# Seven block products for eight: half of the k-tiles of chunk pairs in a two-layer diffusion trunk

## The chip, the cores and the metric

One core of a Trainium2 chip. The metric is device time of one launch in microseconds (us). Matmuls run on TensorE (PE), elementwise work on VectorE (DVE), ScalarE (ACT) and GpSimd (POOL), DMAs are issued by SyncE (SP).

## The reference

640 tokens (128 context, 512 latent) of 2048 features go through two layers. Each layer modulates the RMS-normed tokens, projects them to several streams, mixes them in two branches, multiplies by a SiLU gate, projects back and adds the residual:

```python
shift, scale, gate = jnp.split(jax.nn.silu(cond) @ ada_w[l] + ada_b[l], 3, axis=-1)
h = rms_norm(x, norm_g[l]) * (1.0 + scale) + shift
y = mixer(h @ w_in)            # layer 0: windowed attention || gated linear attention
                               # layer 1: neighbourhood attention || spatial-gating MLP
x = x + gate * ((y * silu(gp)) @ w_out[l])
...
return rms_norm(x, final_norm_g)
```

The projections are 2048 to 5664 (layer 0), 2048 to 7168 (layer 1) and 2048 to 2048 (each output projection).

## The kernel before

Activations lie with features on partitions: 16 k-tiles of 128 features by 640 tokens. Each fp32 value is kept as a high and a low part (`ah`, `al`), each weight likewise (`whi`, `wlo`). A *chunk* is 128 output features. `mm_k` runs one k-tile of it: hi x high, hi x low, lo x high, each for two halves of 320 tokens, the first with two more columns in front for the shift (322). A chunk is thus 16 x 6 = 96 matmuls; `chunk` runs them and then evacuates the two PSUM banks `pj`. There are 133 chunks: 45 into layer 0 (one of 96 rows), 16 out of it, 56 into layer 1 and 16 out. All activation matmuls are issued at line 334, plain fp32 transposes at 339, the start's at 803; DVE, ACT and POOL instructions go through a recorder and all carry line 187.

Weights come as 512 KB loads of 8 k-tiles (`wraw`; 256 KB for the first chunks). ACT rounds them to `whi`, POOL subtracts to get `wlo`, in a ring of three such units (`wpump`).

The order on every engine is fixed when the program is built: a planner (`Pace`) keeps a clock per engine, `tick` runs after each k-tile and advances tasks (attention heads, evacuations, splits), `need(flag)` stands for a point where the next work of TensorE requires a task to be done. `ada_task` is the lowest task: it computes the modulation rows of the later parts on DVE, a multiply-and-sum of 512 columns of weights against one of two condition rows, both in SBUF (`adas`).

Where one layer's output is the next one's input, the last two and the first two chunks are run by `pair`: both chunks for one half of the tokens, then both for the other, with weights kept in an extra pool (`tphi`, `tplo`). The very last pair splits the tokens at 352 (`LAST`) instead of 320, so that its second half is shorter; `final` then computes the last norm of each half.

After layer 0's windowed attention come its eight last gates, then the first output projection, then layer 1: the MLP's `u` chunks, its `v` chunks, the first two gates, 24 chunks for eight neighbourhood heads, 14 gates, the last output projection. Small products (attention scores, transposes) use four other banks, `sm`.

## Time and profile before

| | us |
|---|---|
| median of three runs | 2222.53 (2221.79 to 2223.55) |
| the profiled execution, its own time | 2221.39 |
| its span, first to last instruction | 2219.6 |
| mean granted TensorE clock | 0.994 |

A group row reads: line, engine, operation, output<-inputs, shape, count | busy us, mean ns of one | idle time of the engine just before, and what ended it. Matmul rows overlap, so the spacing of their starts says more than their length.

### The profile page before, as it was taken

The page shows a single profiled execution, that of the slowest core. Times are in us where ns is not written, and L with a number is a line of the kernel's source. Part 1 is how long each engine was busy: PE and PEld are TensorE (multiplying, and loading weights), DVE is VectorE, ACT ScalarE, POOL GpSimd, SP SyncE. Part 2 cuts the span into 40 slices and gives each one's busy share as a digit, 9 for nine tenths or more (in the row PEclk, how much of TensorE's full clock was granted, in tenths as well). Part 3 has the DMA queues.
Part 4 walks back from the last instruction along what each step waited for, and adds up shares of the span by engine and source line. Part 5 has one row for each costly group of instructions (what it writes and reads, how often), then busy time and mean ns, then how long its engine had stood idle before and what let it go on. Part 6 is the DMA issues. An engine that isn't in the chain of part 4 may idle for free.

```text
span 2219.6 us, 36587 instructions
## 1 busy us (share of the span) xinstructions
PE 2166.6 (98%) x14770; PEld 2094.9 (94%) x14770; DVE 1171.6 (53%) x2525; ACT 714.6 (32%) x1403; POOL 767.9 (35%) x375
## 2 busy tenths in 40 slices
PE   7999999999999999999999999999999999999996
PEld 4789999899899899999999999999999999999996
DVE  1348788887878787978778814222222221140004
ACT  4334344343333334122522222233233322242222
POOL 3433233223222143556433332222323323334453
PEclk9999999999999999999999999999999999999998
DMA  9944343335334243666445522222222222222333
GB/s 374 348 159 128 126 139 104 113 126 174 102 112 131 93 144 121 200 218 200 144 147 191 185 67 76 82 73 81 77 89 75 79 67 75 87 82 88 100 103 114
DMA packets 116377, 288.26 MB, mean 130 GB/s; under 512 B 13232, under 2 KB 25328, under 8 KB 116208
## 3 DMA queue, kind: packets, MB, share of 16 engines
q1 hardware_dynamic: 114736, 284.49, 38.9%
q8 instruction: 116, 1.90, 0.3%
q10 hardware_dynamic: 1472, 1.43, 0.2%
q14 instruction: 53, 0.43, 0.1%
HBM read 270.39 MB, written 12.86 MB: 128 GB/s over the span
## 4 chain that ended last, share of the span: by engine, by line
PE 82%; DVE 9%; issue 3%; DMA 3%; ACT 2%; SPq 1%; POOL 0%; DVEq 0%; ACTq 0%; POOLq 0%
PE pj L334 69%; PE sm L334 10%; DVE adas L187 3%; DVE arena L187 3%; PE sm L339 2%; DVE Y L187 2%; PE sm L803 2%; ACT arena L187 1%; DMA Y<-ada 1%; SPq L364 1%; DMA adas<-crow_s 1%; DMA arena<-xT 0%; DMA wraw<-w_even 0%; DMA adas<-ada 0%; DVE actl L187 0%
## 5 line engine op out<-in xcount | busy, mean ns | idle before, releaser
L187 POOL TENSOR_TENSOR wlo<-wraw,whi 128x1024 fp32r<-128x1024 f32 (+2 forms) x260 | 630.1, 2425 | 1157.4 <-ACT whi L187 979.4
L334 PE MATMUL pj<-acth,whi 128*128 128x322 f32 (+1 forms) x3824 | 919.0, 317 | 1.1 <-DVE Y L187 1.1
L334 PE MATMUL pj<-actl,whi 128*128 128x322 f32 (+1 forms) x3824 | 894.5, 310 | 0.0
L334 PE MATMUL pj<-acth,wlo 128*128 128x322 f32 (+1 forms) x3824 | 894.3, 310 | 0.0
L334 PEld LDWEIGHTS pj<-acth,whi 128*128 128x128 f32 x3824 | 644.5, 190 | 5.3 <-issue 1.7
L334 PEld LDWEIGHTS pj<-acth,wlo 128*128 128x128 f32 x3824 | 649.1, 189 | 0.0
L334 PEld LDWEIGHTS pj<-actl,whi 128*128 128x128 f32 x3824 | 646.7, 189 | 0.1
L187 ACT ACTIVATE whi<-wraw 128x1024 fp32r<-128x1024 f32 (+2 forms) x260 | 262.2, 1010 | 331.9 <-issue 179.0
L187 DVE TENSOR_TENSOR arena<-pj,rstd 128x320 f32<-128x320 f32 (+2 forms) x190 | 77.0, 442 | 406.9 <-ACT bc L187 405.3
L187 DVE CUSTOM_DVE_ANT_0 adas<-adas,part 128x512 bf16<-128x512 f32 x192 | 224.2, 1168 | 19.5 <-DMA adas<-crow_s 7.8
L187 DVE CUSTOM_DVE_ANT_0 adas<-adas,partg 128x512 bf16<-128x512 f32 x192 | 213.0, 1109 | 20.9 <-DMA adas<-crow_s 14.5
L187 DVE SCALAR_TENSOR_TENSOR Y<-pj,G,arena 128x128 f32<-128x128 f32 (+3 forms) x96 | 36.9, 433 | 211.7 <-PE pj L334 210.9
L187 ACT ACTIVATE arena<-arena,bc 128x128 f32<-128x128 f32 (+4 forms) x189 | 97.6, 529 | 110.0 <-DVE arena L187 109.9
L187 ACT ACTIVATE bc<-pj 128x2 f32<-128x2 f32 (+1 forms) x101 | 16.9, 168 | 360.2 <-PE pj L334 352.6
L334 PE MATMUL sm<-arena 128*128 128x128 f32 (+5 forms) x552 | 116.9, 337 | 0.4
L187 DVE CUSTOM_DVE_ANT_0 adas<-adas 128x512 bf16<-128x512 f32 x128 | 110.8, 866 | 11.7 <-DMA adas<-ada_g 7.1
L187 POOL TENSOR_TENSOR arena<-arena 128x320 f32<-128x320 f32 (+2 forms) x58 | 58.6, 1029 | 156.3 <-ACT arena L187 148.1
L187 ACT ACTIVATE arena<-Y 128x320 f32<-128x320 f32 (+3 forms) x76 | 38.6, 512 | 230.0 <-DVE Y L187 229.9
L334 PEld LDWEIGHTS sm<-arena 128*128 128x128 f32 (+1 forms) x552 | 86.0, 190 | 19.5 <-issue 10.6
L187 ACT ACTIVATE arena<-arena,nm 128x384 f32<-128x384 f32 (+3 forms) x80 | 46.8, 584 | 171.7 <-DVE nm L187 171.7
L187 DVE CUSTOM_DVE_ANT_0 arena<-sm,arena 128x384 f32<-128x384 f32 (+3 forms) x80 | 41.2, 515 | 69.4 <-PE sm L334 69.0
L339 PE MATMUL sm<-ident,arena 128*128 128x128 f32 (+1 forms) x382 | 61.0, 274 | 12.7 <-DVE arena L187 7.3
(140 smaller groups left out, 1841.3 us busy)
## 6 DMA issues: line engine op xcount, KB each, us to landing
wraw<-w_odd SPq DMA_DIRECT2D x112, 512.0 KB, 3.7
wraw<-w_even SPq DMA_DIRECT2D x74, 512.0 KB, 3.8
adas<-ada_g SPq DMA_DIRECT2D x128, 256.0 KB, 3.6
adas<-ada SPq DMA_DIRECT2D x128, 256.0 KB, 4.0
wraw<-w_out SPq DMA_DIRECT2D x64, 512.0 KB, 3.8
Y<-ada SPq DMA_DIRECT2D x37, 512.0 KB, 6.8
more<-ada SPq DMA_DIRECT2D x27, 512.0 KB, 7.1
wraw<-w_even SPq DMA_DIRECT2D x28, 256.0 KB, 6.4
```

The source lines that it names most:

```text
L187: return f(*args, **kw)
L334: self.nc.tensor.matmul(out, lhsT, rhs, start=start, stop=stop)
L339: self.nc.tensor.transpose(out, in_, self.ident[:k, :k])
L364: self.nc.sync.dma_start(out, in_)
L803: nc.tensor.matmul(o, c, w[:, j, :], start=(q == 0), stop=(q == 3))
```

## The change

- **Block products.** From the first output projection on, chunks run in pairs (`spair`). Of the 16 k-tiles, 0 to 7 are done as before. Tiles 8 to 11 (J) and 12 to 15 (M) form, with the two chunks and the two token halves, a product of 2 x 2 blocks by 2 x 2 blocks, which is done by Winograd's form of Strassen's algorithm: seven block products (A11, A12, S1, S2, S4, S3, A22) of four k-tiles and three passes each. The weight combinations S1 to S4 are four DVE instructions of 512 columns in a buffer `rs`; the activation combinations T1, T2 and the negated T4 are made once for a layer by `fold` (in `eh`, `el`), T3 replaces the second half of tiles 8 to 11, and `unfold` restores these. Partial sums of products go over a copy (`sums`, ACT) and additions into PSUM (DVE).
- **Boundaries.** `kpair` runs two chunks k-tile by k-tile, the second two tiles behind the first, in an order in which tiles come free early (`LAST`) or are asked for late (`STEPS`); `to_y`, `to_odd` and `fold` work between. The last two chunks are run by halves of 320 (`hpair`), their weights split twice.
- **PSUM.** Eight named banks; large products pick the free bank that is ready first, from four and later five of them. Bank 7 holds the two condition rows for `ada_task` until that is done, whose instructions now take 256 columns and read these rows from PSUM.
- **Weights.** All units have four k-tiles (256 KB, 512 columns), in a ring of five.
- **Order.** Three gate chunks of layer 0 stand among the heads of the second key group. In layer 1 `v` comes before `u`, gates 8 and 9 follow, gates 0 and 1 come after the heads. `Y` tiles 8 to 15 go to DRAM during the neighbourhood attention and come back after it. The neighbourhood mask is part of the bias table, so its DVE addition (128 x 1024 for each head) is gone.

```diff
-LAST = 352
+NS = 4
+SJ = KT - 2 * NS
+CW = 2 + HT
+RING = 2560
 WINDOWS = ((0, 2), (2, 2), (4, 4), (8, 4))
-PIECE = 512
+PIECE = 256
+LAST, STEPS = ((*range(12, 16), *a, *b) for a, b in ((range(8), range(8, 12)), ((*range(4), *range(8, 12)), range(4, 8))))
...
-        self.ps = es.enter_context(tc.tile_pool(name="ps", bufs=4, space=PSUM))
+        self.whl = [self.P([128, RING], n, F32R) for n in ("whi", "wlo")]
+        ps = es.enter_context(tc.tile_pool(name="ps", bufs=1, space=PSUM))
+        self.banks = [ps.tile([128, 512], F32, tag=f"bank{i}", name=f"bank{i}") for i in range(8)]
+        self.npj, self.top, self.held, self.nsm = 4, 8, set(), 0
...
+    def steps(c1, c2):
+        a, b = [[(c, k, 0) for k in range(0, SJ, 4)] for c in (c1, c2)]
+        names = lambda *x: [(c1, f) for f in x]
+        return [*names("A11"), *a[:1], *names("A12"), *a[1:], *names("S1", "S2", "S4"), *b[:1], *names("S3"), *b[1:], *names("A22")]
+    def strassen_jobs(self, c1, c2, last, unit):
+        n, J = NS, self.jobs
+        piece = lambda i, m=1: self.rs[:, 128 * n * i : 128 * n * (i + m)]
+        load = lambda i, c: ("load", lambda: (piece(i, 2), self.chunks[c][0][:, SJ : SJ + 2 * n, :]))
+        add = lambda o, a, b, op: ("add", lambda: (piece(o), piece(a), piece(b)), op)
...
+        after = {
+            "A12": [add(4, 2, 3, ALU.add), add(2, 4, 0, ALU.subtract)],
+            "S2": [add(1, 1, 2, ALU.subtract), add(4, 3, 2, ALU.subtract)],
+        }
...
+    def skew(c1, c2, order):
+        a, b = [(c1, k) for k in order], [(c2, k) for k in order]
+        out = a[:2]
+        for i in range(2, len(order)):
+            out += [a[i], b[i - 2]]
+        return out + b[-2:]
+    def kpair(self, c1, c2, order, ready=None, free=None):
+        for c in (c1, c2):
+            if self.chunks[c][3]:
+                self.chunks[c][3]()
+        banks = {}
+        self.quiet = True
+        for c, k in self.skew(c1, c2, order):
+            if c not in banks:
+                banks[c] = [self.pj(), self.pj()]
+            if self.folded and SJ <= k < SJ + NS:
+                self.need("unfold")
+            if c == c1 and ready:
+                self.need(f"{ready}:{k}")
+            self.mm_k(c, k, [(p, i) for i, p in enumerate(banks[c])], order[0], order[-1])
+            self.kdone(c, k)
+            if c == c2:
+                self.flags.add(f"{free}:{k}")
+            self.tick(3)
+            if k == order[-1]:
+                self.chunks[c][4](*banks[c])
+                self.drop(*banks[c])
+                self.flags.add(f"evac{c}")
+        self.quiet = False
...
+    def hpair(self, c1, c2, after):
         for half in range(2):
             if half:
+                self.need("unfold")
+            for c in (c1, c2):
+                if half == 0 and self.chunks[c][3]:
+                    self.chunks[c][3]()
+                p = self.pj()
+                for k in range(KT):
+                    self.mm_k(c, k, [(p, half)], r=half)
+                    self.kdone(c, k, half)
+                    if k % 2:
+                        self.tick()
+                self.chunks[c][4](*((p, None) if half == 0 else (None, p)))
+                self.drop(p)
+            self.spawn(after(half), first=True)
...
+        def three(out, hi, lo, x, st, sp):
+            h, l = x
+            kw = {"skip_group_check": True}
+            self.mm(out, hi, h, start=st, stop=False, **kw)
+            self.mm(out, hi, l, start=False, stop=False, **kw)
+            self.mm(out, lo, h, start=False, stop=sp, **kw)
...
+        def product(b, view, f, x):
+            hi, lo = self.wget((c1, f))
+            st = first(b)
+            for i in range(NS):
+                three(view(b), hi[:, i, :], lo[:, i, :], x(i), st and i == 0, i == NS - 1)
+                if i % 2:
+                    self.tick()
+            self.wdone((c1, f))
+        def plain(key, a, b):
+            hi, lo = self.wget(key)
+            for i in (0, 2):
+                for p, out, x in ((a, full(a), x1), (b, half(b), x2)):
+                    st = first(p)
+                    for j in (i, i + 1):
+                        three(out, hi[:, j, :], lo[:, j, :], x(key[1] + j), st and j == i, True)
+                    self.tick()
+            self.wdone(key)
+        plus = lambda a, b: nc.vector.tensor_tensor(a, a, b, ALU.add)
+        def copy(a):
+            x = self.sums[:, : a.shape[1]]
+            nc.scalar.activation(x, a, AF.Copy)
+            return x
+        ev1, ev2 = self.chunks[c1][4], self.chunks[c2][4]
+        self.need("T1", "T2", "T4")
+        t, xa = self.pj(), self.pj()
+        xb = v = ya = None
+        for key in self.steps(c1, c2):
+            f = key[1]
+            if len(key) == 3 and key[0] == c1:
+                xb = xb or self.pj()
+                plain(key, xa, xb)
+            elif len(key) == 3:
+                ya = ya or self.pj()
+                plain(key, ya, v)
+            elif f == "A11":
+                product(t, full, f, J(x1))
+                x = copy(full(t))
+            elif f == "A12":
+                product(xa, full, f, M(x1))
+            elif f == "S1":
+                plus(full(xa), x)
+                ev1(xa, None)
+                self.drop(xa)
+                v = self.pj()
+                product(v, full, f, tt(0))
+            elif f == "S2":
+                product(t, full, f, tt(1))
+                x = copy(half(t))
+                plus(x, half(v))
+            elif f == "S4":
+                xb = xb or self.pj()
+                product(xb, half, f, M(x2))
+                plus(half(xb), x)
+                ev1(None, half(xb))
+                self.drop(xb)
+            elif f == "S3":
+                self.need("T3")
+                product(t, half, f, J(x2))
+                x = copy(full(t))
+                self.drop(t)
+            else:
+                ya = ya or self.pj()
+                product(ya, full, f, tt(2))
+                plus(half(v), half(x))
+                plus(full(ya), x)
+                ev2(ya, None)
+                ev2(None, half(v))
+                self.drop(ya, v)
...
+    def fold(self, ready, used, shift=None):
+        nc, Y = self.nc, self.Y
+        self.flags -= {"T1", "T2", "T3", "T4"}
+        one, two = slice(0, HT), slice(HT, T)
+        left = [2, 2]
+        def split(h, l, p):
+            nc.scalar.activation(h, p, AF.Copy)
+            yield
+            yield from self.until(h)
+            yield from self.calm(self.calms[1])
+            nc.vector.tensor_tensor(l, p, h.bitcast(F32), ALU.subtract)
+        def work(w):
+            sub = lambda o, x, y: nc.vector.tensor_tensor(o, x, y, ALU.subtract)
+            if self.folded:
+                yield from self.wait("unfold")
+            yield from self.wait(f"{ready}:{SJ + w}", f"{ready}:{SJ + NS + w}")
+            if w:
+                p = self.pj()
+            else:
+                p = self.sm()
+                self.held.add(self.banks.index(p))
+            q = p[:, :HT]
+            for i in range(w, NS, 2):
+                j, m = SJ + i, SJ + NS + i
+                yield from self.wait(f"{ready}:{j}", f"{ready}:{m}")
+                if shift is not None:
+                    a, u = shift[:, j, :], self.s("fsh", 2)
+                    nc.vector.tensor_tensor(u, shift[:, m, :], a, ALU.subtract)
+                    for f, x, scale in ((0, a, -1.0), (1, a, 1.0), (2, u, 1.0)):
+                        self.split2(self.eh[:, i, f, 0:2], self.el[:, i, f, 0:2], x, scale)
+                sub(q, Y[:, j, two], Y[:, j, one])
+                for f in range(3):
+                    yield from split(self.eh[:, i, f, 2:CW], self.el[:, i, f, 2:CW], q)
+                    if f < 2:
+                        sub(q, Y[:, m, one if f else two], q)
+                yield
+            left[0] -= 1
+            if left[0] == 0:
+                self.flags |= {"T1", "T2", "T4"}
+            for i in range(w, NS, 2):
+                j, m = SJ + i, SJ + NS + i
+                yield from self.wait(f"{used}:{j}")
+                sub(q, Y[:, m, two], Y[:, j, two])
+                yield from split(self.ah[:, j, CW:], self.al[:, j, CW:], q)
+                yield
+            self.drop(p)
+            left[1] -= 1
+            if left[1] == 0:
+                self.flags.add("T3")
+                self.flags.discard("unfold")
+                self.folded = True
+        for w in range(2):
+            self.spawn(work(w))
...
+        cq = two(self.banks[7])
+        todo = []
+        for name, w, tiles, finish, pace in jobs:
             for q in range(D // PIECE):
                 cs = slice(PIECE * q, PIECE * q + PIECE)
+                todo.append((self.d["crow_s"][:, cs].partition_broadcast(128), None))
+                for f in range(0, tiles, 2):
+                    todo.append((w[f : f + 2, :, cs].rearrange("a p b -> p a b"), (name, f, q, pace)))
+            todo[-1] += (finish,)
...
+            if job is None:
+                nc.scalar.activation(cq, raw, AF.Copy)
+                load(i + 3)
+                continue
+            name, f, q, pace = job
+            for j in range(2):
+                for c in range(2):
+                    if j == c == 0:
+                        yield from self.until(cq)
+                    elif j and not c:
+                        load(i + 3)
+                    acc = self.part[name][:, f + j, c : c + 1]
+                    nc.vector.tensor_tensor_reduce(
+                        junk, raw[:, j, :], cq[:, c, :], 1.0, acc if q else 0.0, ALU.mult, ALU.add, acc
+                    )
+                    yield pace
...
+                if kv and h != 5:
+                    i = max(h - 5, 0)
+                    gate_chunk(wE[28 + i], i, (f"ya{i}",), "gx")
...
+        def to_y(l, free, cs):
+            for k in STEPS:
+                yield from self.wait(f"{free}:{k}", *(f"evac{c}" for c in cs if k in (6, 7)))
+                yield from self.until(Y[:, k, :])
+                yield from self.calm(self.calms[0])
+                self.act_plain(k)
+                self.flags.add(f"y{l}:{k}")
+                yield
...
+        def out_proj(l, xsrc, sp):
+            fs = list(range(KT))
+            if l == 0:
+                fs = fs[:6] + fs[8:] + fs[6:8]
+            for i, f in enumerate(fs):
                 pre, ev = self.out_evac(l, f, xsrc, sp)
                 add(wout[l, f], 128, False, pre, ev)
+                if i == 1:
+                    pair("k", STEPS, f"y{l}", f"uo{l}")
+                elif i == KT - 3:
+                    pairs((KT - 4) // 2)
+            do(lambda: self.spawn(self.unfold(), first=True))
...
+            if ct == 1:
+                pair("k", STEPS, "x1", "u1")
+        pairs(3)
...
+            for i in (*range(2, 8), 0, 1):
+                self.dma(ysp[:, i, :], Y[:, 8 + i, :])
...
+        pairs(13)
+        do(open_g1)
+        for n, i in enumerate([2, 3, 4, 5, *range(10, 16)]):
+            gate_chunk(wO[40 + i], i)
+        pairs(5)
+        do(lambda: self.spawn(self.unfold(), first=True))
+        for i in (6, 7):
+            gate_chunk(wO[40 + i], i)
+        cg = pair("k", LAST, None, "fo")
+        k = acts.pop()
+        do(lambda: self.spawn(to_y(1, "fo", cg)))
+        do(lambda: self.fold("y1", "uo1"))
+        acts.append(k)
+        do(lambda: self.need("ada_g1"))
+        out_proj(1, spill, None)
+        pair("h", self.final)
...
-        c = slice(LAST, T) if half else slice(0, LAST)
+        c = slice(HT, T) if half else slice(0, HT)
```

664 lines of the change are left out of this document (388 added, 276 removed).

## The prediction

> **What bounds the kernel now.** I read the busy totals first, then the stages, then the chain in order of time, then TensorE's own waits.
>
> ```profile
> span 2219.6 us, 36587 instructions
> PE 2166.6 (98%) x14770; PEld 2094.9 (94%) x14770; DVE 1171.6 (53%) x2525; ACT 714.6 (32%) x1403; POOL 767.9 (35%) x375
> ```
>
> Busy time by stage (columns: PE, PEld, DVE, ACT, POOL in us, then granted clock, DMA share, GB/s):
>
> ```profile
> 200.00:500.00 300.00, 292.09 (x1999) 287.03 (x1998) 253.09 (x419) 127.25 (x221) 86.00 (x33) 0.99 0.38 123
> 500.00:800.00 300.00, 289.83 (x1896) 276.38 (x1895) 238.20 (x605) 107.04 (x261) 73.40 (x30) 0.99 0.38 122
> 800.00:1300.00 500.00, 498.63 (x3383) 497.74 (x3382) 389.43 (x715) 146.65 (x262) 220.34 (x101) 1.00 0.52 170
> 1400.00:1790.00 390.00, 389.65 (x2593) 376.28 (x2592) 96.76 (x352) 121.37 (x255) 110.32 (x46) 1.00 0.24 78
> 1790.00:2180.00 390.00, 388.59 (x2618) 386.66 (x2617) 60.50 (x131) 100.02 (x170) 159.24 (x82) 1.00 0.27 87
> ```
>
> From 800 to 2180 us TensorE is never without work for more than some tenths of a percent, while DVE falls from 78% to 16%. The chain over that stretch is one row of matmuls after another:
>
> ```profile
> 785.99 277.81 PE pj L334 x1883
> ...
> 1796.75 390.15 PE pj L334 x2634
> ```
>
> 277.81/1883 = 0.1475 us and 390.15/2634 = 0.1481 us for one matmul of 320 or so columns. So from 800 us on, time is the number of these matmuls times 0.148. What remains beside them is small; TensorE's own waits are these:
>
> ```profile
> PE sm L803 <- DMA Y<-ada: 12.4, 5, 6.9
> PE sm L339 <- DVE arena L187: 7.3, 6, 1.4
> PE sm L339 <- DVE Y L187: 3.9, 1, 3.9
> PE sm L339 <- DVE den L187: 3.8, 1, 3.8
> ```
>
> The first is the start-up, which the change leaves; the others lie in the gated linear attention and the windowed attention (200 to 800 us), where the windows leave 7.9 and 10.2 us idle. A wait there costs more than its length:
>
> ```profile
> 394.68 0.33 PE L339 MATMUL sm<-ident,Y 128*128 128x128 f32 x1 [3.86 <-DVE Y L187]
> ...
> 395.45 0.69 PE L334 MATMUL pj<-acth,wlo 128*128 128x322 f32 x2
> 395.94 0.74 PE L334 MATMUL pj<-acth,whi 128*128 128x322 f32 x2
> 396.47 0.73 PE L334 MATMUL pj<-actl,whi 128*128 128x322 f32 x2
> ...
> 398.93 0.47 PE L334 MATMUL pj<-actl,whi 128*128 128x322 f32 x2
> ```
>
> After 3.86 us of idleness two matmuls take 0.53 us (395.94 to 396.47) instead of twice 0.148, from 395.45 to 398.93: 3.5 us at half rate, so 1.7 us are lost on top.
>
> **The change, part by part.**
>
> *Fewer matmuls (the gain).* 133 chunks of 16 k-tiles, two halves and three passes are 12768 matmuls; the changed program's instruction order has 12312. The 456 less are 38 pairs (6 + 6 in the output projections, 3 + 5 + 13 + 5 in the odd layer) times 12: seven products of 4 k-tiles and 3 passes are 84 instead of 96. Widths are 322 and 320 as before, and every matmul still loads its own weights, so I take 456 x 0.148 = 67.5 us, bounds 67.3 (0.1475) and 67.5. Nothing hides it: at these places TensorE sets the time.
>
> *What a block product costs beside it.* Rows by form:
>
> ```profile
> L187 DVE TENSOR_TENSOR Y<-Y,sm 128x320 f32<-128x320 f32 x30 | 14.6, 486 | 43.4 <-PE sm L334 43.4
> L187 DVE TENSOR_TENSOR arena<-arena 128x512 f32<-128x512 f32 x24 | 20.4, 872 | 7.4 <-ACT whi L187 4.5 <-DMA arena<-arena 2.8
> L187 ACT ACTIVATE Y<-sm 128x320 f32<-128x320 f32 x10 | 4.4, 438 | 6.3 <-PE sm L334 6.3
> L187 ACT ACTIVATE whi<-wraw 128x512 fp32r<-128x512 f32 x20 | 12.1, 623 | 21.7 <-PE sm L334 21.7
> L187 POOL TENSOR_TENSOR wlo<-wraw,whi 128x512 fp32r<-128x512 f32 x20 | 25.9, 1304 | 34.6 <-ACT whi L187 32.5 <-PE sm L803 2.1
> ```
>
> Per pair DVE gets five additions of a product (5 x 0.486) and four sums of weights (4 x 0.872): 5.9 us in the 180 x 0.148 = 26.6 us that a pair now takes. ACT gets three copies out of PSUM (1.3 us). There are 11 splits of 512 columns: 11 x 0.623 = 6.9 us on ACT and 11 x 1.304 = 14.3 us on POOL. All of it fits beside the matmuls: DVE has 84% free in the last stage and 22% in the fullest, POOL needs 14.3 of 26.6. The one place within a pair where TensorE comes back for a result is bank `v`: after S1 and S2, ACT copies `t`, DVE adds `v`, and only then may the second chunk's matmuls go on in `v`. The cover is S4 (12 matmuls) and six matmuls into `ya`: 18 x 0.148 = 2.66 us. The hand-off is 0.438 + 0.486 = 0.92 us, so 1.7 us may stand in the two queues; ahead of it in the changed order are at most a split (0.623) on ACT and one or two short instructions on DVE. ACT's copy waits for TensorE with the next pair's splits queued behind it, and POOL and then TensorE wait for those; up to five units of weights stand ready, so a wait of that length starves nobody. I take 0; bounds 0 (covered) and 0.5 us in each of the 38 (19 us). Without any cover it would be 0.92 x 38 = 35 us.
>
> *Modulation rows in PSUM.*
>
> ```profile
> L187 DVE CUSTOM_DVE_ANT_0 adas<-adas,part 128x512 bf16<-128x512 f32 x192 | 224.2, 1168 | 19.5 <-DMA adas<-crow_s 7.8 <-DMA adas<-ada 6.5
> L187 DVE CUSTOM_DVE_ANT_0 adas<-adas,partg 128x512 bf16<-128x512 f32 x192 | 213.0, 1109 | 20.9 <-DMA adas<-crow_s 14.5 <-DMA adas<-ada_g 1.9
> L187 DVE CUSTOM_DVE_ANT_0 adas<-adas 128x512 bf16<-128x512 f32 x128 | 110.8, 866 | 11.7 <-DMA adas<-ada_g 7.1 <-DMA adas<-ada 1.8
> ...
> L187 DVE DVE_READ_ACCUMULATOR2_ANT part<- 128x1 f32 x256 | 20.7, 81 | 0.0
> ...
> L187 DVE CUSTOM_DVE_ANT_0 arena<-sm,arena 128x384 f32<-128x384 f32 x32 | 17.7, 554 | 20.7 <-PE sm L334 20.6
> ...
> L187 DVE CUSTOM_DVE_ANT_0 arena<-sm,arena 128x128 f32<-128x128 f32 x16 | 4.6, 289 | 19.0 <-PE sm L334 19.0
> ```
>
> Before: 224.2 + 213.0 + 110.8 + 2 x 20.7 = 589 us of DVE. After: 1024 pieces of 256 columns; between 289 ns at 128 and 554 at 384 lie 0.42 us, with 0.081 for the accumulator 0.50, so 513 us. The other bound is half of the old mean of 548/512 = 1.07 us, 0.535 + 0.081 = 0.62 a piece, 631 us. I take the first, whose rows have an operand in PSUM as the new form has. DVE wins 76 us (or loses 42), none on the path: it pays for the dozen pairs up to 1300 us (12 x 5.9 = 71 us). The price is a PSUM bank, which leaves three small-product banks instead of four in the attention stages, and two later, until modulation ends. Bounds there: 0, and the same 10.2 us idle once more. I take +1 us.
>
> Why the old form costs 0.87 to 1.17 us where a row with a PSUM operand of 384 columns costs 0.55 is a question for the Trainium skill's "SBUF — State Buffer", section "SBUF: two separate sides": a DVE instruction with two SBUF inputs and a POOL instruction shut each other out for their whole length. By that rule the PSUM operand ends the waiting and modulation costs the 513 us, while the four weight sums of a pair, which have two SBUF inputs, may hold POOL up by 4 x 0.872 = 3.5 us, to 17.8 of its 26.6; without it 631 us would be the likelier figure and the slower rival below a few hundredths more probable. The trace of before can't separate the two.
>
> *Gates between the heads.* Three gate chunks (14.2 us each) move in among the last heads of the windowed attention. Of the 10.2 us idle and the 1.7 us at half rate there I take half back, -6; bounds -12 and 0 (the gate's wait for its head replaces the old one).
>
> *The three layer boundaries.* Between the end of the last pair that runs k-tile by k-tile and the first block product lie 192 matmuls, 28.4 us. In it DVE must do:
>
> ```profile
> L187 DVE TENSOR_TENSOR Y<-Y,arena 128x320 f32<-128x320 f32 x46 | 23.8, 517 | 34.8 <-ACT arena L187 34.8
> L187 DVE TENSOR_TENSOR Y<-arena 128x640 f32<-128x640 f32 x24 | 23.3, 982 | 1.1 <-ACT arena L187 1.1
> ```
>
> eight activation tiles (8 x 0.982 = 7.9), one chunk's evacuation (4 x 0.5 = 2.0), four folded tiles of one SBUF and five PSUM instructions each (4 x (0.517 + 5 x 0.486) = 11.8) and the first weight sums (3.5): 25.2 of 28.4 us, which fits only if nothing waits. At the odd layer come two rstd halves and the shift columns, about 8 us more by the same rows: 33, so 5 us late, and with the stop one half-rate stretch. What is late is the first block product, and with it all of TensorE. The modulation task stands still here, so nothing of it queues ahead. I take 1.5 + 6.7 + 1.5 = 10 us; bounds 0 and 35 (10 us and a half-rate stretch at each).
>
> *Queues and the end.* SP issues 1014 instead of 805 DMAs, weights in pieces of 256 KB, and eight `Y` rows (0.33 MB each) go out and come back around the neighbourhood attention. DMA is busy 24% of that stage, so I count nothing; if the first head's bias load waits behind all eight stores, 2.6 MB at the 170 GB/s of the fullest stage are 15 us, against the 26.6 us of the pair that runs meanwhile.
>
> ```profile
> 2202.19 0.51 DVE L187 SCALAR_TENSOR_TENSOR Y<-pj,G,arena 128x288 f32<-128x288 f32 x1
> ...
> 2207.68 7.49 DVE L187 SCALAR_TENSOR_TENSOR Y<-Y,small,rstd 128x288 f32<-128x288 f32 x11
> ```
>
> The last half has 320 columns instead of 288: a ninth more on 7.49 us and on some 5 us of short instructions ahead of it, +1.5 us; bounds 0 and 3.
>
> *Sum*, against the profiled execution's own 2221.4 us: -67.5 + 0 + 1 - 6 + 10 + 1.5 = -61.0, so 2160.4. That execution is 1.1 us under the median shown (2222.5): forecast **2162 us**.
>
> **The rivals.**
>
> *Clean*: every boundary is hidden and the attention idles no more: 2222.5 - 67.5 - 12 = 2143 us. For it: DVE's 25.2 of 28.4 us at two boundaries. Against: 33 at the third.
>
> *Boundaries twice as bad*: the fold is a chain from DVE to ACT and back (nine hand-offs for a tile, two tiles in a row); with 1 us of queue at each, 18 us come on top, each boundary is 10 us late, and each stop halves the clock for a while: 2222.5 - 67.5 + 35 = 2190 us. For it: full queues; against: both tasks run side by side.
>
> *Slower*: one mechanism, the hand-off over bank `v`. If 1.7 us of queue grow to 4.0 us on ACT and DVE together, each pair loses 4.0 + 0.92 - 2.66 = 2.26 us, 38 of them 86 us: 2222.5 - 67.5 + 86 = 2241 us. It decides the sign from a loss of 1.77 us a pair, which is 3.5 us of queue. For it: DVE is 78% busy from 800 to 1300 us; against: some 25 of the 38 pairs come later, where it is 16 to 25% busy.
>
> *It doesn't do what it says*: the order of the program has the 456 less, so only a dearer matmul could undo it; products that go three in a row into one bank would have to take 0.148 x 96/84 = 0.169 us. The 0.1475 of the row at 785.99 is for matmuls that alternate between two banks, so this stays open: 2222 us.
>
> **How the numbers follow.** Forecast (2150 to 2177) 0.60, clean (below 2150) 0.14, boundaries (2177 to 2205) 0.16, no saving 0.03, slower 0.07. For 8 in 10 the range takes in clean and most of the boundaries: 2142 to 2190. A change under 0.2% (4.4 us) can't be told from none here. Faster: 0.60 + 0.14 + 0.16 = 0.90; same 0.03; slower 0.07.
>
> **What would show it.** Right: one matmul still 0.148 us; a neighbourhood head's period down from three chunks' 42.6 us of matmuls to 39.9; TensorE over 99% busy from the third boundary on; idleness before the first block product, largest at the odd layer. Wrong: `PE bank <- DVE bank` waits spread over all pairs (slower), waits for `whi` or `wlo` (splits too slow), matmul spacing of 0.16 us or more in products, or idleness in 200 to 800 us above the old 18 us.

## The result, and the profile after

| | before | after |
|---|---|---|
| time, median (lowest to highest) | 2221.84 us (2219.56 to 2223.55) | 2226.22 us (2223.03 to 2229.32) |
| after / before, 95% interval | | 1.0022 (1.0015 to 1.0029) |
| span of the profiled execution | 2219.6 us | 2225.2 us |
| mean granted TensorE clock | 0.994 | 0.984 |

The change makes the kernel slower by 0.2%, 64 us above the forecast of 2162. The head of the page after, busy time first:

```profile
span 2225.2 us, 39309 instructions
PE 2126.0 (96%) x14314; PEld 2042.9 (92%) x14314; DVE 1425.8 (64%) x4010; ACT 908.6 (41%) x1974; POOL 954.5 (43%) x739
```

The 456 matmuls are gone (14770 to 14314), but TensorE's busy time fell by 40.6 us instead of 67.5, and its idle time grew from 53.0 to 99.2 us. DVE does 254 us more than before, ACT 194, POOL 187. The same stages as in the prediction (us of PE, PEld, DVE, ACT, POOL, then granted clock, DMA share, GB/s):

```profile
200.00:500.00 300.00, 293.98 (x2016) 287.62 (x2015) 269.62 (x759) 134.69 (x265) 92.19 (x67) 1.00 0.46 138
500.00:800.00 300.00, 282.87 (x1850) 270.75 (x1849) 244.47 (x862) 111.88 (x278) 78.04 (x61) 0.98 0.43 131
800.00:1300.00 500.00, 475.45 (x3135) 466.75 (x3134) 413.87 (x1256) 211.88 (x460) 247.85 (x194) 0.98 0.49 153
1400.00:1790.00 390.00, 387.72 (x2581) 373.87 (x2579) 165.78 (x451) 169.90 (x388) 171.36 (x130) 1.00 0.25 81
1790.00:2180.00 390.00, 379.17 (x2495) 374.86 (x2496) 169.54 (x284) 152.08 (x307) 219.86 (x171) 0.98 0.30 96
```

The stretch from 800 to 1300 us, where TensorE idled 1.4 us before, now idles 24.6; 500 to 800 idles 17.1 instead of 10.2; 1790 to 2180 idles 10.8 instead of 1.4. Only the neighbourhood attention (1400 to 1790) is nearly as full as before (2.3 us idle for 0.4), and 200 to 500 a little fuller. Counted off in the list of matmuls, from one chunk's first to another's, the stages took (us, with what the prediction's matmul price alone would have saved):

| stage | before | after | saving expected |
|---|---|---|---|
| gated linear attention, from the ninth chunk | 314.6 | 312.3 | 0 |
| windowed attention, first key group | 105.1 | 118.7 | 0 |
| second key group and first gates | 260.3 | 258.5 | 0 |
| first output projection | 227.0 | 229.1 | 10.6 |
| odd layer, u, v and two gates | 270.9 | 277.9 | 14.2 |
| neighbourhood heads and two gates | 439.6 | 417.9 | 23.0 |
| the other gates of the odd layer | 170.0 | 167.0 | 8.9 |
| last output projection | 227.6 | 237.7 | 10.6 |

Where a stage has no boundary the saving is nearly there, 21.7 of 23.0 us (e1, below, shows that 4.3 of them come from other parts of the change). Elsewhere it is eaten, and the first key group, which has no product at all, is 13.6 us longer. TensorE's largest waits after (us in total, times, longest):

```profile
PE bank L363 <- ACT arena L192: 15.2, 12, 7.6
PE bank L358 <- ACT whi L192: 12.1, 5, 4.5
PE bank L363 <- DVE arena L192: 9.2, 9, 4.1
PE bank L358 <- DVE arena L192: 8.0, 9, 2.0
```

The longest single wait is in the windowed attention's first key group. In order of time, from the timelines of DVE, ACT and TensorE:

```profile
527.70 0.69 DVE L192 TENSOR_TENSOR Y<-Y,arena 128x512 f32<-128x512 f32 x1 [3.52 <-DMA arena<-Y]
...
529.64 0.47 DVE L192 CUSTOM_DVE_ANT_0 adas<-adas,bank,part 128x256 bf16<-128x256 f32 x1
...
536.98 0.48 DVE L192 CUSTOM_DVE_ANT_0 adas<-adas,bank,part 128x256 bf16<-128x256 f32 x1
537.38 0.88 DVE L192 TENSOR_TENSOR arena<-bank,rstd 128x320 f32<-128x320 f32 x2
...
537.91 1.12 ACT L192 ACTIVATE arena<-arena,bc 128x128 f32<-128x128 f32 x2 [10.63 <-DVE arena L192]
...
538.36 0.47 PE L363 MATMUL bank<-ident,arena 128*128 128x128 f32 x1 [7.61 <-ACT arena L192]
```

DVE waits 3.5 us for a rotation's transfer, and then 15 modulation pieces of 0.53 us stand in a row ahead of the evacuation that ACT has been waiting for, for 10.6 us, and TensorE for 7.6. At the odd layer's boundary it is the unfolding, one tile of four shown, and what waits behind it:

```profile
1080.07 0.50 DVE L192 TENSOR_TENSOR bank<-eh,el 128x320 f32<-128x320 f32 x1
1080.60 0.50 DVE L192 TENSOR_TENSOR bank<-bank,actl 128x320 f32<-128x320 f32 x1
1081.14 0.50 DVE L192 TENSOR_TENSOR bank<-bank,acth 128x320 f32<-128x320 f32 x1
1082.14 0.49 DVE L192 TENSOR_TENSOR actl<-bank,acth 128x320 fp32r<-128x320 f32 x1 [0.51 <-ACT acth L192]
...
1091.52 5.47 POOL L192 TENSOR_TENSOR wlo<-wraw,whi 128x512 fp32r<-128x512 f32 x3 [14.36 <-ACT whi L192]
...
1091.44 0.90 PE L358 MATMUL bank<-acth,whi 128*128 128x320 f32 x2 [4.52 <-ACT whi L192]
```

A tile takes 2.5 us, 0.5 of them DVE waiting for ACT's copy. ACT, in turn, holds the copies, the odd layer's rescaling of tiles and the weight splits in one queue: the splits come last, POOL sits idle for 14.4 us, and TensorE 4.5.

### The profile page after: what moved, and what is told of

It reads as the page before. It is cut to its first block, busy times and chain, and to the rows that moved or that the text cites. A ratio compares the mean times of both kernels' runs of the same rounds, so it can differ in the third digit from the quotient of the medians.

```text
span 2225.2 us, 39309 instructions
## 1 busy us (share of the span) xinstructions
PE 2126.0 (96%) x14314; PEld 2042.9 (92%) x14314; DVE 1425.8 (64%) x4010; ACT 908.6 (41%) x1974; POOL 954.5 (43%) x739
## 5 line engine op out<-in xcount | busy, mean ns | idle before, releaser
L358 PE MATMUL bank<-acth,whi 128*128 128x322 f32 (+2 forms) x3576 | 1019.9, 320 | 24.7 <-ACT whi L192 12.1
L358 PE MATMUL bank<-acth,wlo 128*128 128x322 f32 (+2 forms) x3576 | 990.8, 312 | 8.6 <-POOL wlo L192 4.6
L358 PE MATMUL bank<-actl,whi 128*128 128x322 f32 (+2 forms) x3576 | 988.2, 312 | 0.0
L192 POOL TENSOR_TENSOR wlo<-wraw,whi 128x512 fp32r<-128x512 f32 x371 | 498.4, 1351 | 766.0 <-ACT whi L192 660.9
L358 PEld LDWEIGHTS bank<-acth,whi 128*128 128x128 f32 (+1 forms) x3576 | 647.8, 191 | 44.6 <-ACT whi L192 13.7
L358 PEld LDWEIGHTS bank<-acth,wlo 128*128 128x128 f32 (+1 forms) x3576 | 647.6, 190 | 12.4 <-POOL wlo L192 7.5
L358 PEld LDWEIGHTS bank<-actl,whi 128*128 128x128 f32 (+1 forms) x3576 | 647.8, 190 | 0.2
L192 POOL TENSOR_TENSOR wlo<-rs,whi 128x512 fp32r<-128x512 f32 x266 | 361.0, 1367 | 334.7 <-ACT whi L192 312.4
L192 ACT ACTIVATE whi<-wraw 128x512 fp32r<-128x512 f32 x379 | 232.0, 623 | 199.9 <-PE bank L358 69.1
L192 DVE CUSTOM_DVE_ANT_0 adas<-adas,bank,partg 128x256 bf16<-128x256 f32 x448 | 214.4, 478 | 23.3 <-DMA adas<-ada_g 4.8
L192 DVE CUSTOM_DVE_ANT_0 adas<-adas,bank,part 128x256 bf16<-128x256 f32 x448 | 214.6, 479 | 18.1 <-DMA adas<-ada 5.1
```

Source lines behind the costliest of these rows:

```text
L192: return f(*args, **kw)
L358: self.nc.tensor.matmul(out, lhsT, rhs, start=start, stop=stop, **kw)
```

## The experiments

Times are medians; the kernel before measured 2221.6 to 2221.9 us beside each group, so they can be set against 2226.2 for the changed kernel. Each edit is one of the changed kernel unless another is named.

**Products as plain pairs (e1).**

```diff
-            c = [acts.pop()[1] for _ in range(2 * n)][::-1]
-            acts.extend(("s", (c[i], c[i + 1])) for i in range(0, 2 * n, 2))
+            pass
```

(`fold` and `unfold` do nothing then.)

> The 38 block pairs run as plain pairs of 16 k-tiles each, so there is no folding and no unfolding; everything else of the change stays (two-chunk k-tile pairs at the layer boundaries, small modulation pieces, gates between the heads, the new end). 456 matmuls come back, 67 us at 0.148. Theory 'boundaries': folding and unfolding give most of it back (stages around the three boundaries lost about 45 to 50 us against their forecast), so this kernel needs only 15 to 25 us more than the changed one: 2241 to 2251 us, and its idleness between 1060 and 1160 us and 1940 and 1980 us is mostly gone. Rival 'the rest of the change': the products earn their 67 us nearly whole and the loss is in the attention stages and the end: 2275 to 2290 us.

Measured: 2243.64 us, 1.0100 (1.0083 to 1.0117) of before. Block products with all that they need gain 17 us where their matmuls are worth 67: the theory "boundaries". And the rest of the change, without a single product, costs 22 us against before, where the prediction had it at -3.5 (+1 -6 +1.5). Counted off in the list of matmuls as above, these are mainly 13.1 us in the first key group, 6.9 in the odd layer's u and v and 8.9 in the last output projection, less 3.9 in the second key group and 4.3 in the neighbourhood heads.

**One modulation piece a turn (e2).**

```diff
-        for _ in range(4):
+        for _ in range(1):
             if self.low and not (self.quiet and self.tasks) and ...
```

> The modulation task may issue one piece of 256 columns per turn of the planner instead of up to four. Theory 'burst': the row of 16 pieces on DVE that stood ahead of an evacuation at 530 to 537 us (7.6 us of TensorE idle) and the similar one at 615 us (4.2 us), each followed by 6.8 us at half the clock, come from this catching up: both stalls vanish, 2226 - 12 - 7 = 2207 us, with 2200 to 2214 as bounds. Rival 'DVE is simply full there': pieces only move, other evacuations wait in their place, 2222 to 2230 us.

Measured: 2319.21 us, 1.0440 (1.0425 to 1.0456); both expectations missed. The two waits at 538 and 615 us are gone (the longest such wait is 1.5 us), but the odd layer's modulation comes late, and TensorE waits for the first tiles that are scaled with it:

```profile
PE bank L358 <- ACT acth L192: 98.3, 2, 97.2
```

So the rows of pieces can't just be struck: at one a turn the planner issues them too late. That DVE has no time for them isn't shown by this: from 170 to 1060 us it is busy for 639 of 890 us here, and for 756 in the changed kernel.

**Gates behind the heads again (e3).**

```diff
-                if kv and h != 5:
+                if False:
 ...
-        for i in (3, 4, 5):
+        for i in range(6):
```

> The three gate chunks that stand between the last heads of the windowed attention go back behind the heads; the rest of the change stays. Theory 'gates fill the waits' (the prediction's -6 us): without them the attention idles more, 2229 to 2236 us. Rival 'the gates bring nothing, since DVE's modulation pieces and not the heads set the waits': 2222 to 2229 us, the same as the changed kernel. Rival 'the gates' own evacuations wait': 2212 to 2220 us.

Measured: 2229.91 us, 1.0038 (1.0023 to 1.0053). The medians differ by 3.7 us, and the second key group with its gates takes 262.8 us in the profile for 258.5; the sign is the prediction's, but the interval overlaps that of the changed kernel, so the gain isn't shown beyond doubt.

**The last pair's weights split once (e4).**

```diff
-                for r in range(2):
-                    for c in x[:2]:
-                        for k in (0, 4, 8, 12):
-                            unit(c, k, r)
+                for c in x[:2]:
+                    for k in (0, 4, 8, 12):
+                        unit(c, k)
+                self.kept = x[1]
```

(The chunk `kept` has its splits in `eh` and `el`, and `kdone` follows the second half.)

> In the last pair, which runs half by half, the weights of both chunks are split once and kept for the second half (the second chunk's in the buffers of the folded activations, free by then) instead of being split twice: 8 of 16 splits of 512 columns and 8 of 16 weight loads go. Theory 'the doubled splits': the waits for weights after 2165 us (3.3 + 3.4 + 1.8 us, and some 10 us at half the clock) go, 2226 - 12 = 2214 us, bounds 2210 to 2219. Rival 'the unfolding and the tail's own chain of DVE and ACT set the end': 2222 to 2229 us.

Measured: 2217.58 us, 0.9983 (0.9974 to 0.9992): 8.6 us gained. The old waits after 2165 us are gone, but a new one stands at 2166 us:

```profile
PE bank L358 <- ACT eh L192: 4.6, 1, 4.6
```

The kept chunk's splits queue on ACT behind the unfolding's copies, which wait for DVE.

**An eighth of the modulation (e5).**

```diff
-                    nc.vector.tensor_tensor_reduce(junk, raw[:, j, :], cq[:, c, :], 1.0, acc if q else 0.0, ...)
+                    if not q:
+                        nc.vector.tensor_tensor_reduce(junk, raw[:, j, :], cq[:, c, :], 1.0, 0.0, ...)
```

> Modulation reduces over the first 256 of 2048 columns only (its values are then those of an eighth of the sum): 128 pieces instead of 1024, with the loads, the copies of the row and the PSUM bank kept as they are. Theory 'pieces': the queue of modulation pieces on DVE is what the gated linear and windowed attention lost, and part of what the out projection lost: 2226 - 20 = 2206 us, bounds 2198 to 2212, with the waits at 538 and 615 us gone. Rival 'the lost bank or the changed order of the attention': 2220 to 2228 us, the waits stay.

Measured: 2203.09 us, 0.9916 (0.9901 to 0.9931): 23.1 us gained, as the theory said, with the bank still held. The windows of the attention stages:

```profile
200.00:500.00 300.00, 296.45 (x2037) 290.78 (x2036) 184.65 (x331) 140.65 (x272) 95.24 (x66) 1.00 0.60 182
500.00:800.00 300.00, 293.43 (x1930) 279.69 (x1929) 133.98 (x405) 119.17 (x297) 83.83 (x64) 0.99 0.56 171
```

Idle time between 500 and 800 us falls from 17.1 to 6.6. The first key group takes 110.0 us on three small banks instead of four, 8.7 less than in the changed kernel and still 4.9 more than before. The 23.1 us are what seven eighths of the modulation cost in the changed kernel; the kernel before has to do it too, and no run leaves it out there, so they aren't what the change added.

**Modulation rows in SBUF again, in pieces of 256 (e6).**

```diff
-        cq = two(self.banks[7])
+        cq = two(self.adas[:, 4 * W : 5 * W])
 ...
-            self.top = 7
+            self.top = 8
```

> The modulation rows stay in SBUF (256 columns, as pieces of 256) and the small products have their fourth bank back; the rest of the change stays. Theory of the prediction: with two SBUF operands a piece costs 0.62 us or more instead of 0.52, DVE grows by 100 us or more, the attention stages and the first boundary wait longer: 2234 to 2250 us. Rival 'the bank is worth more than the shorter pieces': 2214 to 2222 us.

Measured: 2343.82 us, 1.0549 (1.0533 to 1.0565): the sign of the prediction's theory, far beyond its size. The pieces by form, and the longest wait:

```profile
L192 DVE CUSTOM_DVE_ANT_0 adas<-adas,partg 128x256 bf16<-128x256 f32 x448 | 321.1, 717 | 11.4 <-ACT adas L192 0.9
L192 DVE CUSTOM_DVE_ANT_0 adas<-adas,part 128x256 bf16<-128x256 f32 x448 | 294.1, 657 | 16.9 <-ACT adas L192 4.0
...
PE bank L358 <- ACT acth L192: 111.3, 2, 110.6
```

With both operands in SBUF a piece takes 657 to 717 ns against 478 to 479 in the changed kernel (rows below), and the modulation comes 111 us late. Counted off piece by piece in the trace, it isn't the operand's place alone: 667 of the 1024 pieces run while GpSimd executes nothing and take a mean of 422 ns (from zero) and 483 ns (with a start value), as with the rows in PSUM; the 357 that overlap a GpSimd instruction take 1.04 to 1.07 us. With the rows in PSUM such an overlap makes no difference (478 and 480 ns). That agrees with the rule of the Trainium skill, "SBUF — State Buffer", section "SBUF: two separate sides", that a DVE instruction with two SBUF inputs and one of GpSimd that reads SBUF shut each other out. Without the rows in PSUM the change would be a loss of 5%.

**Products without folding and unfolding (e7).**

```diff
-        self.flags -= {"T1", "T2", "T3", "T4"}
+        self.flags |= {"T1", "T2", "T3", "T4"}
+        return
 ...
-        for i in range(NS):
+        for i in range(0):
```

> The block products run as they do, but on folded tiles that are filled once with other data after the windowed attention; no folding and no unfolding is done at any boundary (the values are then wrong, the matmuls and their order the same). Theory 'boundaries': without them 25 to 40 us of the loss go, the stages from 876 to 1383 us take 480 to 490 us instead of 507, 2226 - 32 = 2194 us, bounds 2183 to 2204. Rival 'the products themselves or the rescaling of the odd layer's tiles': 2212 to 2228 us.

Measured: 2191.46 us, 0.9869 (0.9853 to 0.9885): 34.8 us gained with every product and its additions still there. The stretch with the first two boundaries, in the changed kernel and here:

```profile
870.00:1390.00 520.00, 495.45 (x3296) 489.37 (x3295) 420.22 (x1226) 216.41 (x468) 274.78 (x213) 0.98 0.48 150
```

```profile
870.00:1390.00 520.00, 508.76 (x3418) 504.11 (x3417) 385.03 (x1140) 211.62 (x443) 283.43 (x220) 0.99 0.50 155
```

24.6 us idle become 11.2.

**The end with a later unfolding (e8)**, on top of e4.

```diff
-            do(lambda: self.spawn(self.unfold(), first=True))
+            do(lambda: self.spawn(self.unfold(), 6.0 * l, first=True))
 ...
-            if half:
-                self.need("unfold")
+                    if half and c == c1 and k == SJ:
+                        self.need("unfold")
```

> As e4 (the last pair's weights split once), and the unfolding before it starts 6 us later and is asked for only at the ninth k-tile of the second half. Theory: the 4.6 us that e4 still waited at 2166 us for a split on ACT, behind the unfolding's copies, and some 5 us at half the clock after it go: 2217.6 - 6 = 2211 us, bounds 2208 to 2214. Rival 'the second half waits for the late unfolding instead': 2216 to 2222 us.

Measured: 2213.87 us, 0.9963 (0.9950 to 0.9976), 12.4 us below the changed kernel. In the last pair TensorE waits for nothing.

**Own sums for the pieces (e9).**

```diff
-                        ..., 1.0, acc if q else 0.0, ALU.mult, ALU.add, acc
+                        ..., 1.0, 0.0, ALU.mult, ALU.add, acc
```

(`acc` is a column of its own for each of the eight parts; they are added at the end.)

> Each modulation piece starts its sum at zero and writes it to a place of its own; six additions over up to 256 columns per table join the eight sums at the end. In the changed kernel a piece that goes on from an earlier sum takes 479 ns and one that starts at zero 418 ns, so 896 x 0.06 = 54 us of DVE go, in an order of the instructions that is nearly the same. Theory 'length of the queue': 2226 - 6 = 2220 us, bounds 2214 to 2223, the piece at 0.42 us wherever it stands. Rival 'the number of pieces ahead, not their length': 2223 to 2228 us. Rival 'the 479 ns are the port and not the form': pieces stay at 0.47 us.

Measured: 2221.21 us, 0.9999 (0.9989 to 1.0008): 5.0 us gained. First the changed kernel's groups by form, then this kernel's:

```profile
L192 DVE CUSTOM_DVE_ANT_0 adas<-adas,bank,part 128x256 bf16<-128x256 f32 x448 | 214.6, 479 | 18.1 <-DMA adas<-ada 5.1 <-ACT bank L192 0.7
L192 DVE CUSTOM_DVE_ANT_0 adas<-adas,bank,partg 128x256 bf16<-128x256 f32 x448 | 214.4, 478 | 23.3 <-DMA adas<-ada_g 4.8 <-ACT bank L192 4.3 <-ACT bc L192 2.7
L192 DVE CUSTOM_DVE_ANT_0 adas<-adas,bank 128x256 bf16<-128x256 f32 x128 | 53.6, 418 | 4.7 <-ACT bank L192 1.4
L192 DVE DVE_READ_ACCUMULATOR2_ANT part<- 128x1 f32 x512 | 42.5, 83 | 0.0
```

```profile
L192 DVE CUSTOM_DVE_ANT_0 adas<-adas,bank 128x256 bf16<-128x256 f32 x1024 | 428.1, 418 | 49.0 <-DMA adas<-ada 7.8 <-ACT bank L192 6.7 <-DMA adas<-ada_g 5.3
```

All 1024 pieces take 418 ns: the 60 ns belong to the form that reads a start value.

**A second plain pair (e10).**

```diff
-                if i == 1:
+                if l == 0 and i == 1:
+                    pair("k", STEPS, f"y{l}")
+                elif i == (1 if l else 3):
                     pair("k", STEPS, f"y{l}", f"uo{l}")
```

(and likewise for v in the odd layer)

> In the first output projection and at the head of the odd layer a second pair runs k-tile by k-tile ahead of the first block product, 24 matmuls more (3.6 us), so that the folding has 57 us of matmuls for cover and not 28. Theory of the prediction 'the first block product is late': the waits at 1142 to 1150 us and before the first product at 877 us go, 2226 + 3.6 - 12 = 2218 us, bounds 2212 to 2223. Rival 'the first plain pair itself waits, for its activation tiles and for weight splits behind the unfolding': these waits stay and the 24 matmuls are paid, 2226 to 2232 us.

Measured: 2226.64 us, 1.0027 (1.0016 to 1.0039), nothing against the changed kernel's 1.0022, and inside the rival's range. The 3.6 us of added matmuls are won back and no more: the waits of 2.0, 3.3 and 2.9 us in the plain pairs (877, 1096 and 1117 us) stay, and one of 2.3 us at 1148 us.

**All three suspects taken away (e11):** the edits of e5, e7 and e8 together.

> Three suspects taken away together: modulation over 256 of 2048 columns (as e5), products on tiles that are filled once, without folding and unfolding (as e7), and the last pair's weights split once (as e8). If the account is complete and the three don't overlap beyond the last stage (e5 -23, e7 -35, and of e8's -12 the 9 that e7 hadn't taken there already), 2226 - 67 = 2159 us, bounds 2152 to 2167: the matmuls saved come out as time. Rival 'they cover the same idleness on DVE, or the products stretch': 2172 to 2190 us.

Measured: 2163.87 us, 0.9745 (0.9730 to 0.9759), 62.4 us below the changed kernel. The head of its page:

```profile
span 2163.0 us, 36958 instructions
PE 2107.6 (97%) x14314; PEld 2031.5 (94%) x14314; DVE 949.2 (44%) x2054; ACT 895.2 (41%) x1918; POOL 951.7 (44%) x735
```

The three nearly add up (23 + 35 + 9 were 67 expected, 62 came, so 5 us are common to two of them), and with the same 14314 matmuls the kernel now ends 58 us ahead of before.

**A mended kernel (e12):** the edits of e8, e9 and e10 together, and in the unfolding

```diff
-            nc.scalar.activation(h, p, AF.Copy)
-            nc.vector.tensor_tensor(self.al[:, j, CW:], p, f(h), ALU.subtract)
+                nc.scalar.activation(self.ah[:, j, CW:], p, AF.Copy)
+            if before:
+                q, k = before
+                nc.vector.tensor_tensor(self.al[:, k, CW:], q, f(self.ah[:, k, CW:]), ALU.subtract)
+            before = p, j
```

> A mended kernel with the reference's arithmetic: own sums per modulation piece (e9), the second plain pair (e10), the last pair's weights split once with the later unfolding (e8), and the unfolding with the next tile's additions ahead of the last tile's rest, so that DVE doesn't wait 0.5 us for ACT in each tile. Theory: 2226 - 6 - 8 - 12 - 2 = 2198 us, bounds 2190 to 2208. Rival 'the second plain pair brings nothing': 2208 to 2216 us.

Measured: 2205.29 us, 0.9929 (0.9914 to 0.9944): faster than before by 16 us, than the changed kernel by 21, 7 short of the theory's 2198.

**The unfolding alone left out (e13).**

```diff
-        for i in range(NS):
+        for i in range(0):
             j = SJ + i
             yield from self.bank()
```

> Only the unfolding is left out (the pairs that run k-tile by k-tile then read folded tiles, so values are wrong); the folding stays. Of the 35 us that e7 gained without both: theory 'unfolding' (it starts while weight splits and the next activation tiles want the same two engines, and isn't in the 25.2 us that the prediction counted for a boundary): it carries 20 us or more, 2226 - 22 = 2204 us, bounds 2196 to 2209. Rival 'folding, as the prediction thought': the unfolding carries 10 us or less, 2216 to 2224 us.

Measured: 2205.89 us, 0.9926 (0.9912 to 0.9941), 20.3 us gained: the unfolding is the larger part, and the folding the other 14.4 (2205.9 to 2191.5). At the odd layer's boundary, where the changed kernel had the 14.4 us of idle POOL and TensorE was busy for 37.3 of 43 us, it is full (a stop of 2.9 us just behind it, at 1111 us there and 1103 us here, stays):

```profile
1057.00:1078.00 21.00, 21.00 (x143) 20.88 (x142) 13.00 (x45) 9.85 (x21) 13.53 (x12) 1.00 0.71 225
...
1078.00:1100.00 22.00, 22.00 (x148) 21.51 (x146) 13.59 (x28) 14.87 (x38) 9.75 (x7) 1.00 0.26 87
```

**The mended kernel without the second plain pair (e14):** e12's edits less e10's.

> The mended kernel e12 without its second plain pair. Theory 'the second plain pair pays only for itself' (e10: 2226.6 against 2226.2): 2205 us as e12, bounds 2201 to 2209. Rival 'in the mended kernel the folding is what is late': 2210 to 2218 us.

Measured: 2207.73 us, 0.9935 (0.9920 to 0.9950). The second pair is worth 2.4 us there, within the intervals.

**The mended kernel with a higher price per piece (e15)**, on top of e12.

```diff
-                a = 0.19 if sbuf > 1 else 0.14
+                a = 0.19 if sbuf > 1 else 0.2
```

> The mended kernel e12, with the planner's price of a modulation piece raised by 0.06 us, towards its measured 0.50 us (0.14 to 0.20 us fixed). Theory 'the rows of pieces ahead of an evacuation come from the low price': the waits at 535 and 615 us shrink from 4 us each, 2205 - 6 = 2199 us, bounds 2193 to 2203. Rival 'the odd layer's modulation then ends too late': 2208 us or more, with a wait before the odd layer.

Measured: 2235.35 us, 1.0060 (1.0043 to 1.0077). The rival holds:

```profile
PE bank L359 <- ACT acth L192: 23.2, 2, 22.2
```

With a price nearer to what a piece takes, the planner spreads them and is 22 us late. The low price is what gets the modulation done in time, at the cost of rows of pieces ahead of others' work. DVE isn't full before the odd layer: from 170 to 1060 us it is busy for 676 of 890 us here. Whether another order would fit the pieces into what is left, no run tried.

## Why the prediction was wrong, point by point

*Fewer matmuls (-67.5).* Right as a count and as a price. 456 went, and a product's matmul isn't dearer: outside the stretches at half rate the median distance from its start to the next is 148 to 149 ns, for the other weight matmuls from 865 us on 147 to 148. The mean lengths agree:

```profile
L358 PE MATMUL bank<-el,whi 128*128 128x322 f32 x312 | 96.8, 310 | 0.0
...
L358 PE MATMUL bank<-actl,whi 128*128 128x322 f32 x1356 | 422.6, 312 | 0.0
```

Not all of the 67.5 us comes out, though (next point).

*Beside a block product (0, bounds 0 and 19): +15, and not by the mechanism named.* The hand-off over `v` isn't what waits. The addition there writes `sums`, so its row would be `PE bank <- DVE sums` (not `DVE bank`, as the prediction has it); the changed kernel has no such wait, e7 one of 0.3 us. The rival that made the kernel slower in this way is out. But e7 against e1, both without folding and unfolding, gains 52.2 us where the matmuls are worth 67.5. Stage by stage the products bring 5.6 of 10.6 us in the first output projection, 9.7 of 14.2 in the odd layer's u and v, 17.2 of 23.0 in the neighbourhood heads, 8.5 of 8.9 in the other gates and all 10.6 in the last output projection. What eats the 15 us is open; e7's waits for `wlo` are 4 us longer than e1's (7.7 for 3.7). A weight sum took more than the forecast's 0.872 us: the 38 that overlap no GpSimd instruction take 0.69, the other 114 1.16.

```profile
L192 DVE TENSOR_TENSOR rs<-rs 128x512 f32<-128x512 f32 x152 | 157.8, 1041 | 133.8 <-DMA rs<-w_odd 65.3 <-POOL wlo L192 47.6 <-DMA rs<-w_out 19.6
```

*Modulation rows in PSUM (+1): the step that failed first in time.* The sum of DVE's time was off by 54 us (214.6 + 214.4 + 53.6 + 2 x 42.5 = 567.6 for 513), because the two rows it went by, at 289 and 554 ns, start from a constant; e9 shows 428.1 + 83.5 = 512. But that size wasn't the mistake: e9 takes the 54 us away and gains 5. The prediction costed the modulation as a total and counted only the lost bank on the path. It passed over what the diff does to the order: pieces half as long with a shorter pace (0.4 for 0.8 in the first two of three tables), and a task that may issue four in a turn and catch up on two microseconds. So pieces come in rows of up to 8 us, in front of the evacuations that the attention waits for. Against before, the first key group is 13.6 us longer, and e5 gives 8.7 of them back; the other 4.9 stay open (the lost bank is one candidate). The two simple ways of spreading the pieces come too late (e2, e15).

The prediction also says that the trace of before can't tell whether SBUF operands are slow in themselves or wait for GpSimd. Counted piece by piece it can: those that overlap no GpSimd instruction take 687 ns (from zero) and 749 (with a start value), those that do 1.4 to 1.8 us.

*Gates between the heads (-6).* The sign fits, -3.7 in e3, but isn't clear of the noise.

*The three layer boundaries (+10, bounds 0 to 35): +35, its far bound.* The 25 and 33 us of DVE work were counted for the folding alone, and only up to the first block product. The unfolding was in the diff (four tiles of four DVE instructions and one copy each, at the end of each output projection and of the odd layer's products), and was costed at nothing; by the prediction's own rows of 0.5 us it is 8 us of DVE, 10 with its waits. It starts as the last products end, where ACT has the next pair's splits and the next tiles to make, and carries 20 of the 35 us: e13's stages are 7.6 us shorter in the first output projection, 5.6 in the odd layer's gates and 9.9 in the last output projection (and 1.5 longer in u and v). The folding carries the other 14, somewhat above the 10 forecast. What is late first is also not "the first block product": at the second and third boundary the waits of 4.5 and 2.2 us for `whi` stand in the plain pair that ends the stage before, which e10's second pair doesn't help.

*The end (+1.5): some 12.* The last half's 320 columns cost no more than was forecast (from the start of the last weight matmul to the end 19.8 us for 19.0). But the last pair now runs half by half and splits its weights twice, 16 splits instead of 8, with the unfolding in the same queues. The prediction named the new end and costed only its tail. Splitting once and unfolding later give back 12.4 us (e8), a part of which e13 and e7 count as unfolding.

*The clock.* The prediction added one half-rate stretch at a boundary. There were ten between the first matmuls and the last pair's end, against three before: mean granted clock 0.984 for 0.994, which over the spans is 36 us for 13 of full-speed time not granted (part of it inside the idle time and the tail). That is most of why TensorE's busy time fell by 40.6 us and not by 67.5: a matmul at half rate is busy for longer. So a stop cost more than each term above allowed for it.

In sum, like for like: from before to e1 the rest of the change costs 21.7 us where -3.5 was forecast, from e1 to e7 the products bring 52.2 us of 67.5, and from e7 to the changed kernel folding and unfolding cost 34.8 us for 10. These are 25, 15 and 25 us, together the 65 us between the forecast -61 and the measured +4. The prediction's own signs of being wrong came too: waits for `whi` and `wlo`, 16.7 us from ACT and POOL where before had none, and 23 us idle from 200 to 800 us for 18.

The rival "boundaries twice as bad" had 35 us for the boundaries, as measured, but that is partly luck: it counted queues within the folding alone, which carries 14 of them, its "10 us late" doesn't follow from its own 18 us on top of 25.2 in 28.4 (that would be 15), and it knew nothing of the other two parts.

Not settled: what takes the 15 us beside the products. A stop at the odd layer's first plain pair, which stands in e11 and with 3.0 us in e1 as well, isn't part of them. TensorE waits there for an evacuation on DVE, which stands behind the split of a tile that ACT is still rescaling:

```profile
1081.55 0.63 PE L358 MATMUL bank<-acth,whi 128*128 128x320 f32 x1 [3.00 <-DVE Y L192]
```

## What to carry to other kernels

Work taken off the bounding engine comes out as time only where the others stay out of its way: cost everything that the saving needs (here the undoing of the folding and the doubled splits), at the moment at which it runs and in the queue in which it stands, not as a share of busy time over the stage. When a background task's pieces change in size or pace, look at how many can stand in a row ahead of a short instruction that the bounding engine waits for. To find where an expected gain went, leave out one suspect at a time and then all of them, and compare like with like: a suspect that the old kernel has too must be left out there as well before its cost counts as that of the change.

## What the runs showed of the hardware

*A stop of TensorE can cost more than its length, even a short one.* From the timeline of the changed kernel at the third boundary:

```profile
1945.69 0.46 PE L358 MATMUL bank<-acth,wlo 128*128 128x322 f32 x2
1948.35 0.90 PE L358 MATMUL bank<-acth,whi 128*128 128x322 f32 x2 [2.20 <-ACT whi L192]
...
1952.15 0.73 PE L358 MATMUL bank<-acth,whi 128*128 128x322 f32 x2
1952.68 0.74 PE L358 MATMUL bank<-actl,whi 128*128 128x322 f32 x2
...
1955.18 0.46 PE L358 MATMUL bank<-acth,whi 128*128 128x322 f32 x2
```

After 2.20 us of idleness two matmuls take 0.53 us (1952.15 to 1952.68) until 1955, where they take 0.30 again: 6.5 us at half rate, 3 us lost on top of the 2.2. The length alone doesn't decide. Two stops of 1.66 and 0.80 us in the changed kernel leave the clock alone (the next matmuls start 0.15 us apart), nearly the same two in e7 are followed by some 3 us at half rate (0.26 us apart), and one of 2.91 us in e13 (at 1103 us) is followed by none, with a mean granted clock of 1.00 from 1103 to 1115 us. First the changed kernel, then e7:

```profile
1252.08 0.41 PE L358 MATMUL bank<-acth,whi 128*128 128x320 f32 x1 [1.66 <-ACT whi L192]
...
1253.43 0.41 PE L358 MATMUL bank<-acth,wlo 128*128 128x320 f32 x1 [0.80 <-POOL wlo L192]
1253.68 0.31 PE L358 MATMUL bank<-acth,whi 128*128 128x320 f32 x1
1253.83 0.31 PE L358 MATMUL bank<-actl,whi 128*128 128x320 f32 x1
```

```profile
1234.08 0.42 PE L358 MATMUL bank<-acth,whi 128*128 128x320 f32 x1 [1.61 <-ACT whi L192]
...
1235.42 0.63 PE L358 MATMUL bank<-acth,wlo 128*128 128x320 f32 x1 [0.79 <-POOL wlo L192]
1235.86 0.47 PE L358 MATMUL bank<-acth,whi 128*128 128x320 f32 x1
1236.12 0.47 PE L358 MATMUL bank<-actl,whi 128*128 128x320 f32 x1
```

The Trainium skill, "TensorE: Matmul & The Clock Gate", section "Why this matters for your kernels", advises against idle gaps over some 3 us between bursts of matmuls; here 2.2 were enough, and 2.9 were not always.

*A reduction that starts from an earlier sum* costs 60 ns more than one that starts at zero (478 for 418 ns at 256 columns), and the read of the accumulator 83 ns beside either, so pieces of 256 columns spend a quarter of their 0.56 us on these two. Neither grows with the columns: in the kernel before, at 512 columns, the difference is 62 ns (687 and 749, over the pieces that overlap no GpSimd instruction) and the read 81.
